# Taking the recurrent gates of two channel chunks together at every second step

## The chip, the cores and the metric

The kernel runs on one core of a Trainium2 chip. The metric is the device time of one execution in microseconds (us). TensorE does the matrix multiplications, VectorE and ScalarE the element-wise work and the evacuation of PSUM, GpSimd a few products, and SyncE's queue issues the loads of the weights. In the rows PE is TensorE, PEld its weight loads, DVE VectorE, ACT ScalarE, POOL GpSimd and SP SyncE.

## What is computed

One decoder layer on 512 tokens of width 1024, in float32. The part that matters here is the recurrent branch:

```python
xc = _causal_conv(x_rnn, conv_w, conv_b)                    # four taps over time
r = sigmoid(einsum('bshi,hij->bshj', xb, w_rg) + b_rg)      # 16 blocks of 64 channels
i = sigmoid(einsum('bshi,hij->bshj', xb, w_ig) + b_ig)
log_a = -8 * r * softplus(-lam)
a = exp(log_a); mult = sqrt(-expm1(2 * log_a))
h = associative_scan(a, mult * (i * xc))
y_a = (h * gelu(g_rnn)) @ w_rnn_proj
```

Beside it there are an attention branch (y_b, whose output projection is done during the recurrent branch), two gates that weigh the branches, an output projection, an MLP with a hidden width of 4096 and a gated embedding at the end.

## The kernel before

Activations lie transposed, 128 channels on the partitions and 512 tokens along the free axis, so 1024 channels are eight chunks of 128. Every weight comes as a unit of 128 x 1024 numbers, enough for one output chunk: `wload` (L123) has three units prepared ahead, and for each new unit SyncE's queue issues a load into `wr`, ScalarE copies it to a rounded `wh` (L118) and VectorE takes the remainder `wl` (L119). One output chunk is 24 matmuls in `proj` (L149): eight inner chunks times three products (wh with the high and the low part of the activation, L145 and L146, and wl with the high part, L147). So the third matmul of a unit is the first that needs its `wl`.

The order of TensorE, ScalarE, SyncE and GpSimd is the order of the program text (`manual_schedule`, L80). VectorE's order is laid out by the framework's scheduler, at build time, from what it expects to be ready. ScalarE has no spare order: an instruction that waits holds everything that the text puts behind it.

The stage that changes is the loop at L692, ten steps m = 0 to 9, with these parts:

- a projection `px{m}` of the recurrent input for m < 8, on TensorE;
- `x_scale` (L621): VectorE takes px out of PSUM into `xb`, ScalarE makes the first tap of the convolution, `xc` (L625);
- from m = 2 on, `gate_unit(m - 2)` (L639): six matmuls of 64 x 128 weights into two PSUM banks of the pair `tr` (two halves of the contraction, 64 rows each, L648), and four sigmoids of 64 x 512 on ScalarE (L654, L655);
- `x_conv` (L628): three taps on VectorE (L632), then the split of xc into a high part (ScalarE, L131) and a low part (VectorE, L132);
- one sigmoid of a gate of the attention branch, or four in steps 8 and 9 (L719);
- from m = 2 on, `wload` and `proj` of `pyb{m-2}`, the attention branch's projection, with `gate_post` (L658: a product on GpSimd, a Tanh on ScalarE) between them.

After every second chunk the pair's Exp stands on ScalarE (`decay_exp`, L665), in the next step its VectorE operations and Sqrt (`decay`, L669), and a step later its scans (L678). Exp, Sqrt and the sigmoids each need another function table on ScalarE (ACT_TABLE_LOAD). The last chunk's gates are taken in step 9 after `pyb7`, right before the loop over the eight projections `pgl{m}` (L737), whose results are multiplied with the scans' outputs.

PSUM has eight banks: four for projections (`mm`), two `tr`, and two in one tile `S` for the attention scores, whose last use is before this loop.

Of the kernel before, what the change touches and what calls it, by code (L numbers as in the profile page):

```python
# [9 lines left out]
F32 = mybir.dt.float32  # L10
F32R = mybir.dt.float32r
AF = mybir.ActivationFunctionType
# [4 lines left out]
P = 128  # L17
S = 512
D = 1024
KC = D // P  # L20
# [21 lines left out]
V_GMIX, V_GMLP, V_GPLE, V_CB, V_BRG, V_BIG, V_LAM, V_CW = 0, 8, 16, 24, 32, 40, 48, 56  # L42
# [8 lines left out]
LAG = 2  # L51
# [19 lines left out]
def layer_kernel(ctx, tc, w_all, x_t, p_t, vecs, row, ctab, out_t):  # L71
    nc = tc.nc
# [19 lines left out]
    def ftile(name):  # L92
        return act.tile([P, S], F32, tag="f", name=name, bufs=F_BUFS)

    def mm_ps(name):
        return ps.tile([P, S], F32, tag="mm", name=name, bufs=4)

    def tr_ps(name):
        return ps.tile([P, S], F32, tag="tr", name=name, bufs=2)
# [9 lines left out]
    def wsplit(u, pool, bufs, parts=1):  # L109
        raw = wp.tile([P, 1024], F32, tag="wr", name=f"wr{u}", bufs=2)  # L110
        wh = pool.tile([P, 1024], F32R, tag="wh", name=f"wh{u}", bufs=bufs)
        wl = pool.tile([P, 1024], F32R, tag="wl", name=f"wl{u}", bufs=bufs)
        n = 1024 // parts
        cuts = [slice(i * n, (i + 1) * n) for i in range(parts)]
        for c in cuts:
            nc.sync.dma_start(raw[:, c], w_all[u][:, c])
        for c in cuts:
            nc.scalar.activation(wh[:, c], raw[:, c], AF.Copy)  # L118
            nc.vector.tensor_tensor(out=wl[:, c], in0=raw[:, c], in1=wh[:, c].bitcast(F32),  # L119
                                    op=ALU.subtract)  # L120
        return wh, wl

    def wload(u):  # L123

        while u not in ready or (order and len(ready) <= AHEAD):
            wissue()
        return ready.pop(u)
# [21 lines left out]
    def proj(out, w, acts, ks=range(KC), kcs=KC, w0=0, t=slice(0, S)):  # L149

        wh, wl = w
        for k in ks:
            c = slice(w0 + k * P, w0 + (k + 1) * P)
            a = chunk(acts, k)
            mm3(out, wh[:, c], wl[:, c], a[:, 0, t], a[:, 1, t], k == 0, k == kcs - 1)
# [19 lines left out]
    def col(v, m):  # L175
        return vec[:, v + m : v + m + 1]
# [53 lines left out]
    def s_ps(name):  # L230
        return ps.tile([P, 4, 256], F32, tag="S", name=name, bufs=1)
# [240 lines left out]
    def p_transpose(u, g):  # L472
        sm, _ = probs[u, g]
        pt = tr_ps(f"ppt{u}{g}")
        for i in range(4):
            nc.tensor.transpose(pt[:, i * P : (i + 1) * P], sm[:, i, :], ident)
        p_t_[u, g] = pt

    def p_evac(u, g):
        pt = p_t_.pop((u, g))  # L480
        n = window(u)[1]
        for kb in range(n):
            prt = ftile(f"pt{u}{g}{kb}")
            if n == 1:
                nc.scalar.activation(prt, pt, AF.Copy)
            else:
                nc.vector.tensor_tensor(out=prt.rearrange("p (i t) -> p i t", t=P),
                                        in0=pt.rearrange("p (i t) -> p i t", t=P),
                                        in1=heads4(keep[kb]), op=ALU.mult)
            p_t_[u, g, kb] = prt  # L490

    def pv(u):
        po = mm_ps(f"po{u}")
        b0, nb = window(u)
        for kb in range(nb):
            for g in range(2):
                kv = 2 * (u // NB) + g
                nc.tensor.matmul(po[g * HD : (g + 1) * HD, :],
                                 vt[:, b0 + kb, kv * HD : (kv + 1) * HD],
                                 p_t_.pop((u, g, kb)), start=kb == 0, stop=kb == nb - 1)  # L500
        return po.rearrange("p (i t) -> p i t", t=P)

    def o_split(u, po):
        t = slice(u % NB * P, (u % NB + 1) * P)
        oj = o[u // NB]
        nc.scalar.activation(oj[:, :, 0, t], po, AF.Copy)
        nc.vector.tensor_tensor(out=oj[:, :, 1, t], in0=po, in1=oj[:, :, 0, t].bitcast(F32),
                                op=ALU.subtract)
# [108 lines left out]
    rnn = None  # L617
    hr = [None] * KC
    conv, gw, batch = {}, [], []

    def x_scale(m, px):  # L621
        xb = ftile(f"xb{m}")
        nc.vector.tensor_tensor(out=xb, in0=px, in1=rb, op=ALU.mult)
        xc = rnn.tile([P, S], F32, tag="h", name=f"xc{m}", bufs=KC)
        nc.scalar.activation(xc, xb, AF.Identity, bias=col(V_CB, m), scale=col(V_CW + 24, m))  # L625
        conv[m] = xb, xc

    def x_conv(m):  # L628
        xb, xc = conv[m]
        for j in range(3):  # L630
            sft = 3 - j
            nc.vector.scalar_tensor_tensor(  # L632
                out=xc[:, sft:], in0=xb[:, : S - sft], scalar=col(V_CW + 8 * j, m),
                in1=xc[:, sft:], op0=ALU.mult, op1=ALU.add)
        xr = rnn.tile([P, 2, S], F32R, tag="xr", name=f"xr{m}", bufs=3)
        split(xc, xr)
        conv[m] = xc, xr

    def gate_unit(m):  # L639


        xc, xr = conv.pop(m)
        halves = [slice(0, HD), slice(HD, P)]
        pgs = [tr_ps(f"pg{m}_{j}") for j in range(2)]
        c = slice(m * P, (m + 1) * P)
        for i, (w, part) in enumerate(((0, 0), (0, 1), (1, 0))):
            for pg, rows in zip(pgs, halves):
                nc.tensor.matmul(pg, gw[w][rows, c], xr[rows, part, :],  # L648
                                 start=i == 0, stop=i == 2)
        r = ftile(f"r{m}")  # L650
        ig = rnn.tile([P, S], F32, tag="ig", name=f"ig{m}", bufs=4)
        for j, pg in enumerate(pgs):
            own, other = halves[j], halves[1 - j]
            nc.scalar.activation(r[own], pg[own], AF.Sigmoid, bias=col(V_BRG, m)[own])  # L654
            nc.scalar.activation(ig[own], pg[other], AF.Sigmoid, bias=col(V_BIG, m)[other])  # L655
        return m, xc, (r, ig)

    def gate_post(m, xc, both):  # L658
        r, ig = both
        nc.gpsimd.tensor_tensor(out=ig, in0=ig, in1=xc, op=ALU.mult)  # L660

        nc.scalar.activation(xc, r, AF.Tanh, scale=cs[:, 0, m : m + 1])
        batch.append((m, r, ig, xc))
# [24 lines left out]
    def att_evac(m, py):  # L688
        nc.vector.tensor_tensor(out=gb[m], in0=py, in1=gb[m], op=ALU.mult)

    py_last = None
    for m in range(KC + LAG):  # L692
        if m < KC:
            w = wload(U_X + m)
            px = mm_ps(f"px{m}")
            proj(px, w, xg, range(0, 4))
            if m == 0:
                p_transpose(7, 1)
                p_evac(7, 1)
            proj(px, w, xg, range(4, 8))  # L700
            if m == 0:
                po = pv(7)
                o_split(7, po)
                att_scope.close()
                rnn = rnn_scope.enter_context(tc.tile_pool(name="rnn", bufs=1))
                gw += wsplit(U_GATE, rnn, 1)
        if py_last:
            att_evac(*py_last)
        for f in later.pop(0):
            f()  # L710
        later.append([])
        if m < KC:
            x_scale(m, px)
        if LAG <= m < KC + LAG - 1:
            g = gate_unit(m - LAG)
        if m < KC:
            x_conv(m)
        for gt in gb[m : m + 1] or ga[4 * (m - KC) : 4 * (m - KC) + 4]:
            nc.scalar.activation(gt, gt, AF.Sigmoid)  # L719
        if m >= LAG:  # L720
            w = wload(U_ATT + m - LAG)
            py_last = m - LAG, mm_ps(f"pyb{m - LAG}")
            if m < KC + LAG - 1:
                gate_post(*g)
            proj(py_last[1], w, o)
            if m == KC + LAG - 1:
                gate_post(*gate_unit(m - LAG))
        if len(batch) == 2:
            pair = list(batch)
            batch.clear()  # L730
            decay_exp(pair)
            later[0].append(partial(decay, pair))
            later[1] += [partial(scan, *p) for p in pair]
# [3 lines left out]
    for m in range(KC):  # L737
        w = wload(U_G + m)
        pg = mm_ps(f"pgl{m}")
# [15 lines left out]
    for m in range(KC):  # L755
        w, py = first[m] if m < 2 else (wload(U_RNN + m), mm_ps(f"pya{m}"))
# [13 lines left out]
    for m in range(KC):  # L770
        w = wload(U_OUT + m)
# [16 lines left out]
    for grp in range(4):  # L788
        us = rtiles(f"u{grp}_")
        for m in range(KC):  # L790
            w = wload(U_MLP + 16 * grp + m)
# [11 lines left out]
        for m in range(KC):  # L803
            w = wload(U_MLP + 16 * grp + 8 + m)
# [9 lines left out]
    for m in range(KC):  # L814
        if m % 4 == 0:
            w = wload(U_PLE + m // 4)
# [11 lines left out]
    for m in range(KC):  # L828
        w = wload(U_PG + m)
        parts = 2 if m == KC - 1 else 1  # L830
        for i in range(parts):
            pg = mm_ps(f"ppg{m}_{i}")
# [87 lines left out]
```

## Time and profile before

| | us |
|---|---|
| median of 3 runs | 849.38 (849.28 to 849.86) |
| the profiled execution, its own time | 850.14 |
| its span, first to last instruction | 847.7 |
| granted TensorE clock, mean | 0.999 |
| TensorE busy | 835.4 |
| VectorE busy | 524.5 |
| ScalarE busy | 363.9 |

The page gives the share of busy time of each engine over the whole span. A timeline gives for each instruction its start and duration in us from the start of the span, and in brackets how long its engine had idled before it and which instruction ended that. The ends of matmuls are modelled, so their starts are what is read.

### The profile page before, as it was taken

How to read it: one execution, taken by the hardware profiler on the slowest of the kernel's cores; microseconds unless marked ns; L12 is line 12 of the kernel's file. 1: busy time of each engine (PE TensorE's matmuls, PEld its weight loads, DVE VectorE, ACT ScalarE, POOL GpSimd, SP SyncE). 2: the span in 40 equal slices, each digit the busy share in tenths (PEclk: the TensorE clock that was granted, in tenths of full speed). 3: DMA queues.
4: the chain of work that ended last, by engine and by line, in shares of the span. 5: the costliest groups of instructions: out<-in, count | busy, mean ns of one | idle time of the engine just before them, and what ended most of it. 6: DMA issues, size and time to landing. Idle time of an engine off the chain costs nothing.

```text
span 847.7 us, 9949 instructions
## 1 busy us (share of the span) xinstructions
PE 835.4 (99%) x3798; PEld 679.7 (80%) x3798; DVE 524.5 (62%) x763; ACT 363.9 (43%) x583; POOL 103.0 (12%) x127
## 2 busy tenths in 40 slices
PE   9999999999999999999999999999999999999997
PEld 7878777777778788888888888888888888888886
DVE  5677787787678858675557633564355435555374
ACT  7334665555488896433343222222222222233431
POOL 2811422232011110000120000000000000002100
PEclk9999999999999999999999999999999999999999
DMA  7334212112233222334433232223322322332231
GB/s 248 124 98 152 70 55 75 50 63 66 71 102 96 77 75 80 118 124 149 140 109 101 98 113 92 95 99 100 100 86 92 121 95 80 99 100 100 75 124 51
DMA packets 25743, 83.99 MB, mean 99 GB/s; under 512 B 3040, under 2 KB 3424, under 8 KB 25696
## 3 DMA queue, kind: packets, MB, share of 16 engines
q1 hardware_dynamic: 25552, 83.32, 29.5%
q8 instruction: 30, 0.49, 0.3%
q14 instruction: 17, 0.14, 0.1%
q10 hardware_dynamic: 144, 0.05, 0.0%
HBM read 80.20 MB, written 2.10 MB: 97 GB/s over the span
## 4 chain that ended last, share of the span: by engine, by line
PE 92%; DVE 3%; DMA 2%; ACT 1%; POOL 1%; issue 1%; SPq 0%; ACTq 0%; POOLq 0%
PE pu L145 7%; PE pd L145 7%; PE pu L146 7%; PE pd L147 7%; PE pd L146 7%; PE pu L147 7%; PE pgate L145 4%; PE pgate L147 3%; PE pgate L146 3%; PE pq L246 2%; DMA wr<-in_w_all 2%; PE pyb L145 2%; PE S L424 2%; PE pgl L145 2%; PE ppg L145 2%; PE ppg L146 2%
## 5 line engine op out<-in xcount | busy, mean ns | idle before, releaser
L119 DVE TENSOR_TENSOR wl<-wr,wh 128x1024 fp32r<-128x1024 f32 (+1 forms) x144 | 180.6, 1256 | 58.3 <-ACT wh L118 58.1
L118 ACT ACTIVATE wh<-wr 128x1024 fp32r<-128x1024 f32 (+1 forms) x144 | 150.2, 1045 | 126.3 <-PE pd L146 98.4
L145 PE MATMUL pu<-x1g,wh 128*128 128x512 f32 x256 | 100.0, 391 | 0.0
L146 PE MATMUL pu<-x1g,wh 128*128 128x512 f32 x256 | 99.6, 389 | 0.0
L147 PE MATMUL pu<-x1g,wl 128*128 128x512 f32 x256 | 99.6, 389 | 0.0
L145 PE MATMUL pd<-u,wh 128*128 128x512 f32 x256 | 99.6, 389 | 0.0
L146 PE MATMUL pd<-u,wh 128*128 128x512 f32 x256 | 99.6, 389 | 0.0
L147 PE MATMUL pd<-u,wl 128*128 128x512 f32 x256 | 99.6, 389 | 0.0
L131 ACT ACTIVATE u<-up 128x512 fp32r<-128x512 f32 x32 | 20.2, 632 | 126.5 <-DVE up L798 126.5
L206 POOL TENSOR_TENSOR sq<-sq,sq_x 128x512 f32<-128x512 f32 x14 | 18.2, 1299 | 455.9 <-ACT sq_x L204 455.9
L807 DVE TENSOR_TENSOR xr<-pd,xr 128x512 f32<-128x512 f32 x32 | 22.1, 691 | 81.4 <-PE pd L147 81.4
L145 PEld LDWEIGHTS pu<-x1g,wh 128*128 128x128 f32 x256 | 48.0, 188 | 10.2 <-issue 0.2
L146 PEld LDWEIGHTS pu<-x1g,wh 128*128 128x128 f32 x256 | 48.1, 188 | 10.1 <-issue 0.2
L147 PEld LDWEIGHTS pd<-u,wl 128*128 128x128 f32 x256 | 48.0, 188 | 10.1
L147 PEld LDWEIGHTS pu<-x1g,wl 128*128 128x128 f32 x256 | 48.0, 188 | 10.1
L145 PEld LDWEIGHTS pd<-u,wh 128*128 128x128 f32 x256 | 48.0, 188 | 9.9
L146 PEld LDWEIGHTS pd<-u,wh 128*128 128x128 f32 x256 | 48.0, 188 | 9.9
L145 PE MATMUL pgate<-xg,wh 128*128 128x512 f32 x128 | 51.4, 402 | 0.0
L147 PE MATMUL pgate<-xg,wl 128*128 128x512 f32 x128 | 50.2, 392 | 0.0
L146 PE MATMUL pgate<-xg,wh 128*128 128x512 f32 x128 | 50.0, 391 | 0.0
L797 DVE TENSOR_TENSOR up<-pu,rb_x 128x512 f32<-128x512 f32 x32 | 22.1, 691 | 40.0 <-PE pu L147 40.0
L468 POOL TENSOR_SCALAR sm<-sm,st 128x128 f32<-128x128 f32 x64 | 30.1, 488 | 100.7 <-DVE st L466 45.6
(217 smaller groups left out, 1634.6 us busy)
## 6 DMA issues: line engine op xcount, KB each, us to landing
wr<-in_w_all SPq DMA_DIRECT2D x142, 512.0 KB, 3.3
x<-in_x_t SPq DMA_DIRECT2D x8, 256.0 KB, 5.1
xr<-in_x_t SPq DMA_DIRECT2D x8, 256.0 KB, 3.6
out<-pgt SPq DMA_DIRECT2D x7, 256.0 KB, 2.0
kt<-kt SPq DMA_DIRECT2D x8, 128.0 KB, 2.3
wr<-in_w_all SPq DMA_DIRECT2D x2, 256.0 KB, 3.3
pk<-in_p_t SPq DMA_DIRECT2D x2, 256.0 KB, 3.7
tab<-in_ctab SPq DMA_DIRECT2D x1, 384.0 KB, 6.6
```

The lines of the kernel that those rows point to most:

```text
L118: nc.scalar.activation(wh[:, c], raw[:, c], AF.Copy)
L119: nc.vector.tensor_tensor(out=wl[:, c], in0=raw[:, c], in1=wh[:, c].bitcast(F32), op=ALU.subtract)
L131: nc.scalar.activation(r[:, 0, :], src, AF.Copy)
L145: nc.tensor.matmul(out, ah, bh, start=start, stop=False)
L146: nc.tensor.matmul(out, ah, bl, start=False, stop=False)
L147: nc.tensor.matmul(out, al, bh, start=False, stop=stop)
L206: nc.gpsimd.tensor_tensor(out=acc, in0=acc, in1=t, op=ALU.add)
L246: nc.tensor.matmul(banks[n], a[:, part, n * P : (n + 1) * P], w[:, c], start=k == 0 and i == 0, stop=k == KC - 1 and i == 2)
L424: nc.tensor.matmul(pss[:, i, :], q_t[u][:, i % 2, 2 * g + i // 2, :], kt[part][:, kv, b0 * P : b0 * P + 256], start=part == 0, stop=part == 1)
L468: nc.gpsimd.tensor_scalar(out=sm[:, i, :], in0=sm[:, i, :], scalar1=den[:, i : i + 1], scalar2=1.0, op0=ALU.mult, op1=ALU.mult)
L797: nc.vector.tensor_tensor(out=y, in0=pu, in1=r1, op=ALU.mult)
L807: nc.vector.tensor_tensor(out=x1[m], in0=pd, in1=x1[m], op=ALU.add)
```

## The change

Where the loop took the gates of chunk m - 2 in each step from 2 to 9, it takes those of chunks m - 3 and m - 2 in the steps 3, 5, 7 and 9. All twelve matmuls stand together, then all eight sigmoids. The first chunk of a pair keeps the two `tr` banks, the second has the two banks of the score tile. The two calls of `gate_post` follow where the one stood. In step 9 the gates stand ahead of `pyb7`, where the last chunk's stood behind it.

```diff
-    def gate_unit(m):
+    def gate_units(ms):
-        xc, xr = conv.pop(m)
         halves = [slice(0, HD), slice(HD, P)]
-        pgs = [tr_ps(f"pg{m}_{j}") for j in range(2)]
-        c = slice(m * P, (m + 1) * P)
-        for i, (w, part) in enumerate(((0, 0), (0, 1), (1, 0))):
-            for pg, rows in zip(pgs, halves):
-                nc.tensor.matmul(pg, gw[w][rows, c], xr[rows, part, :],
-                                 start=i == 0, stop=i == 2)
-        r = ftile(f"r{m}")
-        ig = rnn.tile([P, S], F32, tag="ig", name=f"ig{m}", bufs=4)
-        for j, pg in enumerate(pgs):
...
-        return m, xc, (r, ig)
+        wide = s_ps(f"pg{ms[1]}").rearrange("p a b -> p (a b)")
+        banks = [[tr_ps(f"pg{ms[0]}_{j}") for j in range(2)], [wide[:, 0:S], wide[:, S : 2 * S]]]
+        units = []
+        for m, pgs in zip(ms, banks):
+            xc, xr = conv.pop(m)
+            c = slice(m * P, (m + 1) * P)
+            for i, (w, part) in enumerate(((0, 0), (0, 1), (1, 0))):
+                for pg, rows in zip(pgs, halves):
+                    nc.tensor.matmul(pg, gw[w][rows, c], xr[rows, part, :],
+                                     start=i == 0, stop=i == 2)
+            units.append((m, xc, pgs))
+        done = []
+        for m, xc, pgs in units:
+            r = ftile(f"r{m}")
+            ig = rnn.tile([P, S], F32, tag="ig", name=f"ig{m}", bufs=4)
+            for j, pg in enumerate(pgs):
+                own, other = halves[j], halves[1 - j]
+                nc.scalar.activation(r[own], pg[own], AF.Sigmoid, bias=col(V_BRG, m)[own])
+                nc.scalar.activation(ig[own], pg[other], AF.Sigmoid, bias=col(V_BIG, m)[other])
+            done.append((m, xc, (r, ig)))
+        return done
...
-        if LAG <= m < KC + LAG - 1:
-            g = gate_unit(m - LAG)
+        units = gate_units((m - 3, m - 2)) if m > LAG and m % 2 else []
...
-            if m < KC + LAG - 1:
+            for g in units:
                 gate_post(*g)
             proj(py_last[1], w, o)
-            if m == KC + LAG - 1:
-                gate_post(*gate_unit(m - LAG))
```

## Rows read from the trace of the kernel before

**Rows 1.** The page, busy time of each engine over the span.

```profile
PE 835.4 (99%) x3798; PEld 679.7 (80%) x3798; DVE 524.5 (62%) x763; ACT 363.9 (43%) x583; POOL 103.0 (12%) x127
```

**Rows 2.** Windows, two stretches: length, then busy us (count) of PE, PEld, DVE, ACT, POOL.

```profile
270.40:294.40 24.00, 24.00 (x109) 18.61 (x107) 20.65 (x26) 20.50 (x28) 3.10 (x3) 1.00 0.27 88
294.40:307.40 13.00, 13.00 (x62) 9.97 (x61) 10.38 (x14) 12.84 (x19) 2.33 (x2) 1.00 0.13 40
```

**Rows 3.** TensorE's timeline at chunk 0's gates, and the first matmul of pyb2.

```profile
227.58 0.39 PE L147 MATMUL px<-xg,wl 128*128 128x512 f32 x1
227.90 0.50 PE L648 MATMUL pg<-xr,wh 64*128 64x512 f32 x2
228.24 0.40 PE L648 MATMUL pg<-xr,wh 64*128 64x512 f32 x2
228.47 0.40 PE L648 MATMUL pg<-xr,wl 64*128 64x512 f32 x2
228.80 0.50 PE L145 MATMUL pyb<-o,wh 128*128 128x512 f32 x1
229.14 0.40 PE L146 MATMUL pyb<-o,wh 128*128 128x512 f32 x1
...
252.79 0.50 PE L145 MATMUL pyb<-o,wh 128*128 128x512 f32 x1
```

**Rows 4.** TensorE's timeline: start of pyb7, third matmuls of pgl1 and of pgl4.

```profile
300.91 0.39 PE L145 MATMUL pyb<-o,wh 128*128 128x512 f32 x1
...
313.36 0.39 PE L147 MATMUL pgl<-xg,wl 128*128 128x512 f32 x1
...
329.68 0.41 PE L147 MATMUL pgl<-xg,wl 128*128 128x512 f32 x1
```

**Rows 5.** VectorE's timeline there: wl of pgl1, evacuation of pyb6, wl of pgl4.

```profile
308.95 1.22 DVE L119 TENSOR_TENSOR wl<-wr,wh 128x1024 fp32r<-128x1024 f32 x1 [2.46 <-ACT wh L118]
310.10 0.68 DVE L689 TENSOR_TENSOR gate<-pyb,gate 128x512 f32<-128x512 f32 x1
...
328.32 1.21 DVE L119 TENSOR_TENSOR wl<-wr,wh 128x1024 fp32r<-128x1024 f32 x1
```

**Rows 6.** ScalarE's timeline at the end of the loop: chunk 7's Tanh, pgl4's wh.

```profile
316.62 0.72 ACT L662 ACTIVATE xc<-r,cs 128x512 f32<-128x512 f32 x1 [1.40 <-POOL ig L660]
...
326.66 1.04 ACT L118 ACTIVATE wh<-wr 128x1024 fp32r<-128x1024 f32 x1
```

**Rows 7.** ScalarE's timeline: wh of pyb2, L625 of the chunks 3, 4, 5 and 7.

```profile
238.77 1.06 ACT L118 ACTIVATE wh<-wr 128x1024 fp32r<-128x1024 f32 x1 [0.47 <-DMA wr<-in_w_all]
241.72 0.82 ACT L625 ACTIVATE xc<-xb,vec 128x512 f32<-128x512 f32 x1 [1.89 <-DVE xb L623]
...
254.87 0.81 ACT L625 ACTIVATE xc<-xb,vec 128x512 f32<-128x512 f32 x1 [0.84 <-DVE xb L623]
...
256.99 0.69 ACT L654 ACTIVATE r<-pg,vec 64x512 f32<-64x512 f32 x1
...
259.82 0.63 ACT L131 ACTIVATE xr<-xc 128x512 fp32r<-128x512 f32 x1
...
266.02 0.82 ACT L625 ACTIVATE xc<-xb,vec 128x512 f32<-128x512 f32 x1 [2.35 <-DVE xb L623]
...
290.30 0.81 ACT L625 ACTIVATE xc<-xb,vec 128x512 f32<-128x512 f32 x1 [2.35 <-DVE xb L623]
```

**Rows 8.** VectorE's timeline: wl of pyb2, xb of chunk 3, taps of chunks 4 and 5.

```profile
239.86 1.23 DVE L119 TENSOR_TENSOR wl<-wr,wh 128x1024 fp32r<-128x1024 f32 x1 [0.92 <-ACT wh L118]
241.01 0.68 DVE L623 TENSOR_TENSOR xb<-px,rb_x 128x512 f32<-128x512 f32 x1
...
258.99 0.74 DVE L632 SCALAR_TENSOR_TENSOR xc<-xb,vec,xc 128x511 f32<-128x511 f32 x1
...
263.03 2.35 DVE L119 TENSOR_TENSOR wl<-wr,wh 128x1024 fp32r<-128x1024 f32 x2
...
266.87 2.32 DVE L632 SCALAR_TENSOR_TENSOR xc<-xb,vec,xc 128x509 f32<-128x509 f32 x3 [0.89 <-ACT xc L625]
```

More of the change, by code (lines that the diff above doesn't have):

```diff
@@ L637, in x_conv @@
         conv[m] = xc, xr
-    def gate_unit(m):
-        xc, xr = conv.pop(m)
+    def gate_units(ms):
         halves = [slice(0, HD), slice(HD, P)]
-        pgs = [tr_ps(f"pg{m}_{j}") for j in range(2)]
-        c = slice(m * P, (m + 1) * P)
-        for i, (w, part) in enumerate(((0, 0), (0, 1), (1, 0))):
-            for pg, rows in zip(pgs, halves):
-                nc.tensor.matmul(pg, gw[w][rows, c], xr[rows, part, :],
-                                 start=i == 0, stop=i == 2)
-        r = ftile(f"r{m}")
-        ig = rnn.tile([P, S], F32, tag="ig", name=f"ig{m}", bufs=4)
-        for j, pg in enumerate(pgs):
-            own, other = halves[j], halves[1 - j]
-            nc.scalar.activation(r[own], pg[own], AF.Sigmoid, bias=col(V_BRG, m)[own])
-            nc.scalar.activation(ig[own], pg[other], AF.Sigmoid, bias=col(V_BIG, m)[other])
-        return m, xc, (r, ig)
+        wide = s_ps(f"pg{ms[1]}").rearrange("p a b -> p (a b)")
[19 more added lines that the diff above has]
+        return done
     def gate_post(m, xc, both):
```

## The prediction

> **What bounds the kernel now.** I read the page first: TensorE is busy for 835.4 of 847.7 us, so at first sight only its own work counts [rows 1]. Then the windows over the loop that is changed. TensorE is busy in all of it, at the full clock, but ScalarE is busy for 20.50 of 24.00 us in two steps of the loop, and for 12.84 of 13.00 at the loop's end [rows 2]. So there are two things to follow: what the change does for TensorE, and whether ScalarE, which prepares TensorE's weights, can still keep up.
>
> TensorE's timeline gives the first. Its plain step is the distance from the third matmul of pgl1 to that of pgl4, three units of 24 matmuls: (329.68 - 313.36)/72 = 0.2267 us [rows 4]. Around a gate unit, 1.56 us pass from the last matmul of px to the second of pyb (227.58 to 229.14) where two plain steps would take 0.45 [rows 3]. A gate unit so costs 1.11 us. Its six matmuls run as three pairs, which start 0.34 and 0.23 apart, so the work itself is 3 x 0.2267 = 0.68, and 0.43 go into the passage from 128-row to 64-row weights and back.
>
> The second comes from the timelines at the loop's end. The wl of pgl4 is finished by VectorE at 328.32 + 1.21 = 329.53 [rows 5], and the matmul that needs it starts at 329.68 [rows 4]: no slack at all. For pgl1 the slack is 313.36 - 310.17 = 3.2 us. In the middle of the loop there is plenty: the wl of pyb2 is ready at 241.09 [rows 8], and pyb2 starts at 252.79 [rows 3]. So whatever moves the wl of pgl4 later moves everything later, since TensorE has no idle time behind it in which to catch up; and TensorE can't keep a gain from the loop unless that wl comes earlier too.
>
> **The change part by part.**
>
> *TensorE.* Eight gate units with two passages each become four. With the second chunk's three pairs at 0.23 each, a double unit costs 1.11 + 0.68 = 1.79, and the saving is 4 x 0.43 = 1.7 us. If the passage from one chunk to the next cost as much as the first step after a passage (0.34 instead of 0.23 for each of three pairs [rows 3]), it would be 1.7 - 4 x 0.33 = 0.4. I take 1.7: the weights change between any two pairs as they do between the chunks. Two steps of the loop then take 4 x 24 x 0.2267 + 1.79 = 23.55 us instead of 23.98.
>
> *What costs nothing by itself.* The score tile's two banks have been free since the attention stage. No load is moved on SyncE's queue, and the matmuls wait for nothing new: chunk m - 3 is a step older than it was. The count of table loads stays at three in two steps, because the sigmoid of L719 stands in the even steps too. The GpSimd products come in pairs, but the Tanh that needs the second stands behind a gate sigmoid, a wh and the first Tanh. In step 9 this even removes a wait: chunk 7's Tanh waited 1.40 for its product [rows 6].
>
> *ScalarE.* Here is the price. From the L625 of chunk 3 to that of chunk 5, two steps, there are 266.02 - 241.72 = 24.30 us, with two waits of 0.84 and 2.35: 21.11 us of work, which the change only rearranges [rows 7]. What it rearranges are the covers. After L625, ScalarE must not do the split (L131) before VectorE has made three taps of the convolution. In an even step of before, the four sigmoids (256.99 to 259.82, 2.83 us) and their table load stand between the two and fill that time; the taps end at 258.99 + 0.74 = 259.73, and the split starts at 259.82 without a wait [rows 7, 8]. After the change nothing stands between them in even steps, so ScalarE waits for the taps, and behind the split are queued the gate sigmoid and the two wh of the next units. Call this wait W. Its lower bound is three taps alone, 2.32 and a hand-over, about 2.35 (as in step 5 [rows 8]); the upper one is the even step of before, where scans stand between the taps: 259.73 - 255.68 = 4.05 [rows 7, 8]. I take 4.05: the Sqrt of the pair still comes right before L625 in the even steps, so the scans become ready just then, as before.
>
> The odd steps have a wait X in front of L625, 2.35 before, because xb stood behind two wl on VectorE [rows 7, 8]. Afterwards px5 ends earlier and the two wh come later, so in order of readiness xb goes first and X is 0; if VectorE keeps its order, X stays at up to 2.35. I take 0. The start of the chain, A, is the L625 of chunk 3: 241.72 as before, if xb still stands behind the wl of pyb2 [rows 8], or 239.83, the end of that wh [rows 7]. I take 241.72, because that wl comes first in the program.
>
> *The sum.* L625 of chunk 7 then starts at B = A + 2 x (21.11 + W + X) = 241.72 + 2 x 25.16 = 292.04, instead of 290.30. From there to the end of the wl of pgl4 there were 329.53 - 290.30 = 39.23 us [rows 5, 7]. Four sigmoids and a Tanh of chunk 4, which stood ahead of B, now stand behind it (2.83 + 0.72), and the wait of 1.40 is gone [rows 6]: 41.38. The wl of pgl4 is ready at 292.04 + 41.38 = 333.42, 3.9 us later than before, and TensorE, which arrives 1.7 us earlier, stands still for some 5.6 us on the way, the first of it (about 1 us) at pgl1. TensorE's saving is then paid out in waiting. The profiled execution is at 850.14 (span 847.7 and 2.44 around it), 0.76 above the median; against the median the forecast is 849.38 + 3.9 = 853.3.
>
> The bounds by the same sum: B can't be before px7 is done. In before px7 ended at 287.87 (252.79 and 0.11, two units to the gates of chunk 3, and 23.98); five gate units of 1.11 ahead of it become two of 1.79, 1.97 less, and xb takes 0.68: 286.7. That gives 286.7 + 41.38 - 329.53 = -1.4. With A = 239.83 and the rest as taken it is +2.0; with X = 2.35 and A = 241.72, B = 296.74 and +8.6.
>
> **The rivals.**
>
> *The saving arrives.* If VectorE makes the taps without scans between them (W = 2.35) and takes xb at once, ScalarE needs 23.46 us for two steps, no more than TensorE's 23.55. From A = 239.83, B is then 286.75, and the time 848.0, at best 847.7 if TensorE keeps all of its 1.7. For it speaks that VectorE's order is laid out anew; against it that even steps of before have scans between the taps [rows 8]. It decides at B = 288.15, where the wl of pgl4 is as early as before. The Trainium skill, TensorEngine Tiling (Array Packing), section Tiling Modes, Key Properties, says that a change of the tiling mode drains TensorE: by that rule alone, half the changes give the whole 1.7 us. The trace agrees on the passages (0.43 each); what the page leaves out is who feeds TensorE afterwards.
>
> *VectorE keeps its order.* X stays at 2.35 and the time becomes 849.38 + 6.6 to 8.6 = 856.0 to 858.0. For it speaks that this order is not one of real readiness: at 308.95 VectorE had stood for 2.46 us before the wl of pgl1 [rows 5], while the evacuation of pyb6 stood behind it, whose matmuls were over when pyb7 began at 300.91 [rows 4]. The scheduler expects ScalarE earlier than it is. Against it: px5 is done 1.5 us earlier.
>
> *The passages don't get fewer in effect.* If TensorE saves only 0.4, the wl of pgl4 still sets the time: 853.3 again.
>
> **How the numbers follow.** The forecast, ScalarE late by 2 to 6 us (851.1 to 855.5): 0.50. VectorE's old order (855.5 to 858): 0.20. The saving arrives (847.5 to 849.4): 0.18. In between (849.4 to 851.1, from a shorter W or an early A): 0.12. About 0.2%, 1.7 us, is what a measurement here can tell from no change. TensorE's whole saving is just that, so of the 0.18 I put 0.07 below 847.7. Same holds the rest of it and the in-between, 0.23; slower 0.70. The range, 848.6 to 857.6, leaves out the best part of the saving and the latest case.
>
> **What would show it.** TensorE: four groups of twelve L648 matmuls, each about 1.8 us. ScalarE: the splits of chunks 4 and 6 wait about 4 us for L632, L625 comes 25 us apart, and that of chunk 7 lies near 292. TensorE's first matmuls with wl in pgl1 to pgl4 wait, 5 to 6 us together. Wrong would be: those splits wait 2.4 or less, or B is before 288.2, or VectorE takes scans ahead of xb.

## The result, and the profile after

The changed kernel takes 853.95 us (median of five runs, 852.83 to 854.23) against 849.38 (five runs, 849.09 to 849.86): a ratio of 1.0052, 95% interval 1.0041 to 1.0063. It is slower by 4.57 us where 3.9 were forecast. The profiled execution took 854.07 us with a span of 852.2.

The page of the kernel after, busy time of each engine and the chain that ended last:

```profile
PE 836.0 (98%) x3798; PEld 680.0 (80%) x3798; DVE 521.3 (61%) x763; ACT 364.1 (43%) x583; POOL 101.4 (12%) x127
...
PE 79%; ACT 8%; DVE 7%; DMA 3%; issue 2%; POOL 1%; SPq 0%; ACTq 0%; POOLq 0%
```

The first line hardly differs from [rows 1]: seen over the whole span, nothing happened. The second does. On the page of before this second line was:

```profile
PE 92%; DVE 3%; DMA 2%; ACT 1%; POOL 1%; issue 1%; SPq 0%; ACTq 0%; POOLq 0%
```

8% of the chain, some 68 us, now run over ScalarE, which is idle for 57% of the span; TensorE's share fell from 92 to 79%. So the loop is to be read by stretches.

Windows of the kernel after, with the columns of [rows 2] (behind POOL stand the granted clock, the DMA share and GB/s):

```profile
270.40:294.40 24.00, 24.00 (x111) 19.37 (x110) 18.48 (x25) 20.21 (x28) 2.59 (x2) 1.00 0.16 52
294.40:307.40 13.00, 12.39 (x59) 9.42 (x58) 8.26 (x13) 12.82 (x18) 2.96 (x2) 1.00 0.34 115
307.40:317.50 10.10, 10.10 (x45) 8.06 (x44) 6.19 (x8) 9.96 (x16) 1.88 (x2) 1.00 0.16 53
317.50:321.50 4.00, 1.39 (x6) 0.53 (x5) 1.23 (x1) 3.98 (x7) 0.70 (x1) 1.00 0.00 0
321.50:325.00 3.50, 3.50 (x9) 2.71 (x9) 1.71 (x4) 3.47 (x5) 0.00 (x0) 0.52 0.42 153
```

ScalarE (the fourth of the five) is full from 294.40 to 325.00: its gaps sum to 0.18 + 0.14 + 0.02 + 0.03 us. TensorE stands still for 0.61 in the second stretch and for 2.61 in the fourth, and in the fifth its granted clock is at 0.52.

TensorE's timeline after: one double gate unit, the double unit of step 9, and the places in pgl1, pgl2 and pgl4 where a matmul came late:

```profile
285.59 0.39 PE L147 MATMUL px<-xg,wl 128*128 128x512 f32 x1
285.91 0.73 PE L651 MATMUL pg<-xr,wh 64*128 64x512 f32 x4
286.48 0.40 PE L651 MATMUL pg<-xr,wl 64*128 64x512 f32 x2
286.71 0.62 PE L651 MATMUL pg<-xr,wh 64*128 64x512 f32 x4
287.18 0.40 PE L651 MATMUL pg<-xr,wl 64*128 64x512 f32 x2
287.50 0.50 PE L145 MATMUL pyb<-o,wh 128*128 128x512 f32 x1
287.84 0.40 PE L146 MATMUL pyb<-o,wh 128*128 128x512 f32 x1
...
300.41 0.50 PE L651 MATMUL pg<-xr,wh 64*128 64x512 f32 x2 [0.61 <-DVE xr L132]
...
312.67 0.50 PE L147 MATMUL pgl<-xg,wl 128*128 128x512 f32 x1
...
320.05 0.50 PE L145 MATMUL pgl<-xg,wh 128*128 128x512 f32 x1 [2.08 <-ACT wh L118]
320.39 0.39 PE L146 MATMUL pgl<-xg,wh 128*128 128x512 f32 x1
321.31 0.51 PE L147 MATMUL pgl<-xg,wl 128*128 128x512 f32 x1 [0.53 <-DVE wl L119]
321.64 0.60 PE L145 MATMUL pgl<-xg,wh 128*128 128x512 f32 x1
322.04 0.63 PE L146 MATMUL pgl<-xg,wh 128*128 128x512 f32 x1
322.47 0.63 PE L147 MATMUL pgl<-xg,wl 128*128 128x512 f32 x1
...
334.03 0.50 PE L147 MATMUL pgl<-xg,wl 128*128 128x512 f32 x1
```

TensorE's own part came true: from 285.59 to 287.84 pass 2.25 us, which is 1.80 more than two plain steps. Its losses come later. Counted from start to start, beyond a plain step for each matmul, they are 0.88 in step 9, 0.25 at pgl1, 3.15 at pgl2, 1.58 in eight matmuls that start some 0.42 apart instead of 0.23 (321.64 to 325.03), and 0.24 at pgl4: 6.10 in all. From the last px matmul of chunk 2 to the last matmul of the program it is 614.99 us in [rows 3]'s execution (227.58 to 842.57) and 619.43 here (227.57 to 847.00): 4.44 more, which is 6.10 less a saving of about 1.7.

ScalarE's timeline after, with the rows that answer to [rows 6] and [rows 7]:

```profile
231.89 0.80 ACT L625 ACTIVATE xc<-xb,vec 128x512 f32<-128x512 f32 x1
...
241.28 0.82 ACT L625 ACTIVATE xc<-xb,vec 128x512 f32<-128x512 f32 x1 [1.89 <-DVE xb L623]
...
261.17 0.63 ACT L131 ACTIVATE xr<-xc 128x512 fp32r<-128x512 f32 x1 [3.48 <-DVE xc L632]
...
267.73 0.82 ACT L625 ACTIVATE xc<-xb,vec 128x512 f32<-128x512 f32 x1 [2.08 <-DVE xb L623]
...
287.77 0.63 ACT L131 ACTIVATE xr<-xc 128x512 fp32r<-128x512 f32 x1 [3.57 <-DVE xc L632]
...
292.15 0.81 ACT L625 ACTIVATE xc<-xb,vec 128x512 f32<-128x512 f32 x1
...
318.95 1.04 ACT L118 ACTIVATE wh<-wr 128x1024 fp32r<-128x1024 f32 x1
```

The split of an even step, which did not wait in [rows 7], now waits 3.48 and 3.57 us for the taps. Chunk 7's L625 starts at 292.15 instead of 290.30, and at 318.95 comes the wh of pgl2 for which TensorE has been standing.

VectorE's timeline after (answering to [rows 5] and [rows 8]): xb in steps 5 and 7, and the wl of pgl2 and pgl4:

```profile
264.73 2.36 DVE L119 TENSOR_TENSOR wl<-wr,wh 128x1024 fp32r<-128x1024 f32 x2 [0.20 <-ACT wh L118]
267.01 0.68 DVE L623 TENSOR_TENSOR xb<-px,rb_x 128x512 f32<-128x512 f32 x1
...
291.05 0.67 DVE L623 TENSOR_TENSOR xb<-px,rb_x 128x512 f32<-128x512 f32 x1
291.63 2.35 DVE L119 TENSOR_TENSOR wl<-wr,wh 128x1024 fp32r<-128x1024 f32 x2
...
320.03 1.23 DVE L119 TENSOR_TENSOR wl<-wr,wh 128x1024 fp32r<-128x1024 f32 x1 [6.21 <-ACT wh L118]
...
332.76 1.22 DVE L119 TENSOR_TENSOR wl<-wr,wh 128x1024 fp32r<-128x1024 f32 x1
```

In step 5 xb still stands behind two wl, in step 7 ahead of them, but behind two scans (at 287.59 and 289.91), though px7's last matmul began at 285.59. The wl of pgl4 is ready at 333.98, 4.45 later than in [rows 5].

### The profile page after: what moved, and what is told of

Its sections match the earlier page's. It is cut to its first block, busy times and chain, and to the rows that moved or that the text cites. A ratio compares the mean times of both kernels' runs of the same rounds, so it can differ in the third digit from the quotient of the medians.

```text
span 852.2 us, 9944 instructions
## 1 busy us (share of the span) xinstructions
PE 836.0 (98%) x3798; PEld 680.0 (80%) x3798; DVE 521.3 (61%) x763; ACT 364.1 (43%) x583; POOL 101.4 (12%) x127
## 4 chain that ended last, share of the span: by engine, by line
PE 79%; ACT 8%; DVE 7%; DMA 3%; issue 2%; POOL 1%; SPq 0%; ACTq 0%; POOLq 0%
PE pu L147 7%; PE pd L147 7%; PE pu L145 7%; PE pd L146 7%; PE pd L145 7%; PE pu L146 7%; PE pgate L145 4%; PE pgate L147 3%; PE pgate L146 3%; PE pq L246 2%; DVE wl L119 2%; DMA wr<-in_w_all 2%; ACT wh L118 2%; PE S L424 2%; PE ppg L147 2%; PE ppg L145 2%
```

## The experiments

The theory, Q: TensorE gets its saving, but ScalarE's queue runs late, because the split waits for taps that nothing covers any more, and TensorE gives the saving back, and more, waiting for weights in pgl. The rivals: T, that TensorE itself loses by the double units; E, that only the new place of the last gates, at the loop's end, costs. Behind the change itself, the first four kernels ran on one chip, the next four on another, the last four on a third, each with its own runs of the kernel before. The last column is the account of TensorE as above, from the profiled executions: the distance from the last px matmul of chunk 2 to the program's last matmul, less the 614.99 of before.

| kernel | us | before, same chip | ratio, 95% | TensorE's distance |
|---|---|---|---|---|
| the change | 853.95 | 849.38 | 1.0052 (1.0041 to 1.0063) | +4.44 |
| cover | 854.89 | 849.46 | 1.0062 (1.0050 to 1.0075) | +5.91 |
| old_end | 855.18 | 849.46 | 1.0068 (1.0054 to 1.0082) | +5.96 |
| last_pair | 848.55 | 849.46 | 0.9992 (0.9983 to 1.0001) | -0.48 |
| order_only | 857.23 | 849.46 | 1.0091 (1.0077 to 1.0105) | +8.14 |
| mm_only | 851.55 | 849.70 | 1.0024 (1.0015 to 1.0034) | +2.22 |
| late_ga | 850.65 | 849.70 | 1.0018 (1.0009 to 1.0027) | +1.04 |
| cover_late_ga | 851.85 | 849.70 | 1.0027 (1.0016 to 1.0037) | +2.66 |
| before_late_ga | 849.18 | 849.70 | 0.9998 (0.9989 to 1.0007) | -0.06 |
| pinned | 849.91 | 849.35 | 1.0005 (0.9996 to 1.0014) | +0.46 |
| pinned_late_ga | 847.72 | 849.35 | 0.9978 (0.9969 to 0.9987) | -1.75 |
| mm_only_late_ga | 847.95 | 849.35 | 0.9981 (0.9972 to 0.9989) | -1.21 |
| before_plus | 851.04 | 849.35 | 1.0020 (1.0011 to 1.0029) | +2.22 |

**cover.** In even steps the convolution's taps and split move behind the weights' preparation, so that work stands on ScalarE between L625 and the split again.

```diff
-        if m < KC:
+        if m < KC and (m % 2 or m < LAG):
             x_conv(m)
...
             py_last = m - LAG, mm_ps(f"pyb{m - LAG}")
+            if m < KC and m % 2 == 0:
+                x_conv(m)
```

> The changed kernel, but in even steps the split of the convolution (and its three taps) stands behind the gate sigmoid and the wh of the next unit in program order; nothing else differs. Theory Q (ScalarE's queue is late because the taps are no longer covered in even steps, and the wl of pgl4 hands that on): ScalarE's waits for L632 in steps 4 and 6 fall from 3.5 us to under 1, L625 of chunk 7 starts at 286.8 to 288.5 instead of 292.15, and the time is 1.4 below to 0.5 above the kernel before (848.0 to 849.9). Rival T (TensorE itself loses: the double gate units in the score banks, its wait of 0.6 for the split of chunk 7, its clock at half speed): no change, 853.5 to 854.5. Rival E (the loss is made only at the loop's end, by the eight sigmoids ahead of the wh of pgl2): no change, about 854.

Q's number was missed, and by the number alone T and E, which expected about 854, come closer. The edit did half of what it was for, W fell to 1.11 in both even steps, but another wait took its place. ScalarE's timeline of this kernel in steps 4 and 5, and VectorE's ahead of xb:

```profile
260.81 0.64 ACT L131 ACTIVATE xr<-xc 128x512 fp32r<-128x512 f32 x1 [1.11 <-DVE xc L632]
266.73 0.82 ACT L625 ACTIVATE xc<-xb,vec 128x512 f32<-128x512 f32 x1 [4.34 <-DVE xb L623]
```

```profile
264.17 0.68 DVE L688 TENSOR_TENSOR ig<-xc,ig 128x512 f32<-128x512 f32 x1
264.89 1.23 DVE L689 TENSOR_TENSOR_SCAN xc<-r,ig 128x512 f32<-128x512 f32 x1
266.04 0.66 DVE L623 TENSOR_TENSOR xb<-px,rb_x 128x512 f32<-128x512 f32 x1
```

The scheduler put a scan and its product ahead of xb, in step 7 too (4.33). From chunk 2's L625 to chunk 7's pass 293.07 - 231.33 = 61.74 us, against 292.15 - 231.89 = 60.26 after the change and 58.40 before (290.30 - 231.90): the queue got later, and with it the kernel. The line of before that belongs to this, the L625 of chunk 2:

```profile
231.90 0.80 ACT L625 ACTIVATE xc<-xb,vec 128x512 f32<-128x512 f32 x1
```

**old_end.** Pairs in the steps 3, 5 and 7; chunk 6 alone in step 8, chunk 7 alone behind pyb7 as before. A single unit takes the two `tr` banks.

```diff
-        units = gate_units((m - 3, m - 2)) if m > LAG and m % 2 else []
+        units = []
+        if m in (3, 5, 7):
+            units = gate_units((m - 3, m - 2))
+        elif m == 8:
+            units = gate_units((6,))
...
             proj(py_last[1], w, o)
+            if m == KC + LAG - 1:
+                for g in gate_units((7,)):
+                    gate_post(*g)
```

> Chunks 0 to 5 in pairs as in the changed kernel, chunks 6 and 7 singly and where they stood before (step 8, and behind pyb7). Theory Q: the queue is as late as in the changed kernel when chunk 7's L625 comes (292.15); behind it come 39.23 us as before and chunk 4's sigmoids and Tanh (3.55): wl of pgl4 at 334.9, so 5 above the kernel before, 854 to 855.5. Rival E: the step-9 sigmoids are back behind the wh of pgl2, so the time is that of the kernel before less three saved passages, 848 to 849.4. Rival T: three quarters of the loss, about 852.8.

With the old end the kernel is still slow, and the number is Q's, but not in Q's way. The wl of pgl4 is about as late as Q had it (334.53), but no matmul waits for it: TensorE had lost its time earlier, in front of the single gate units, whose two PSUM banks ScalarE has not yet emptied (the view of waits from 222 to 335):

```profile
ACT xr L131 <- DVE xc L632: 16.9, 5, 3.6
...
PE pg L653 <- ACT ig L663: 4.6, 4, 1.9
```

The bank waits are of this edit's own making, so this run doesn't clear the new place of the last gates. The next one does.

**last_pair.** The opposite: single units in the steps 2 to 7, one pair in step 9.

```diff
-        units = gate_units((m - 3, m - 2)) if m > LAG and m % 2 else []
+        units = []
+        if LAG <= m < KC:
+            units = gate_units((m - 2,))
+        elif m == KC + LAG - 1:
+            units = gate_units((6, 7))
```

> Chunks 0 to 5 singly as in the kernel before, only chunks 6 and 7 as a pair in step 9. Theory Q: L625 of chunk 7 stays at 290.3, the wl of pgl4 is earlier by the product's wait of 1.4, and TensorE keeps one saved passage: 0.4 below the kernel before, 848.6 to 849.4. Rival E: all or most of the loss, 852 to 854. Rival T: a quarter of the loss, about 850.5.

Where the even steps keep their cover, a double unit and its banks cost nothing: TensorE does not wait in pgl, and its distance shortens by 0.48, one passage (0.43 by the prediction). Step 9 has the change's double unit and its eight sigmoids, so E, which put the loss there (852 to 854), falls. By the median the gain of 0.9 us can't be told from none.

**order_only and mm_only.** Two halves of the change. order_only has the six matmuls of one chunk in each step and the eight sigmoids of a pair in the odd steps; mm_only has the twelve matmuls in the odd steps and four sigmoids in each step, the second chunk's a step later. For both, `gate_units` is split into its matmuls (`gate_mm`, whose second argument picks the score banks) and its sigmoids (`gate_sig`); of each edit only the part in the loop is shown.

```diff
 # order_only
+        if LAG <= m < KC + LAG:
+            held.append(gate_mm(m - 2, m % 2 == 1))
+        if m % 2 and m > LAG:
+            units = [gate_sig(*g) for g in held]
+            held.clear()
 # mm_only
+        if m > LAG and m % 2:
+            held += [gate_mm(m - 3, False), gate_mm(m - 2, True)]
+        if m > LAG:
+            units = [gate_sig(*held.pop(0))]
+        if m == KC + LAG - 1:
+            units.append(gate_sig(*held.pop(0)))
```

> ScalarE's order as in the changed kernel (eight sigmoids in the steps 3, 5, 7, 9), but the matmuls of each chunk's gates in a step of their own as before (the odd-numbered chunks in the score banks), so that TensorE has eight passages again. Theory Q: as slow as the changed kernel, 853.3 to 855, since the saved passages were paid out in waiting. Rival T: like the kernel before, 849 to 850. Rival E: about 854.

> TensorE as in the changed kernel (twelve matmuls in the steps 3, 5, 7, 9), but four sigmoids in each step: the first chunk of a pair in the odd step, the second in the even step after it; chunks 6 and 7 both in step 9. Theory Q: the taps are covered again, L625 of chunk 7 comes at 289 to 291, and behind it stand chunk 4's sigmoids and Tanh (3.55 us) less the product's wait (1.4): 1 to 3 above the kernel before, 850.4 to 852.4. Rival T: as the changed kernel, 853.5 to 854.5. Rival E: as the changed kernel, since step 9 is the same.

order_only is the slowest of all, though it has single units like before: T, by which it should have been no slower than before, falls. But it is no clean half: VectorE took the two wl ahead of xb in both odd steps (X 2.08 twice), W was 4.00 and 3.92, and TensorE got a wait of its own for a bank:

```profile
296.17 0.79 PE L650 MATMUL pg<-xr,wh 64*128 64x512 f32 x1 [2.81 <-ACT ig L661]
```

So its 857.23, above Q's range, shows that the sigmoids' order with what it draws after it costs more than the whole loss, and not which share of the change's loss it is. In mm_only no split waits from chunk 3 on, and chunk 7's L625 comes 56.45 after chunk 2's (287.45 - 231.00), 288.34 on the scale of the change's trace and so a little earlier than Q's 289 to 291; the stall that is left is the wl of pgl4 (1.62) and the wh and wl of pgl2 (0.84 and 0.53). Its number is Q's. TensorE's double units and step 9 are the change's here, so T and E, by which it should have taken 853.5 or more, both miss.

**late_ga and its kin.** Four sigmoids in each of the steps 8 and 9, for the gates `ga` that are needed only in the later loop over pya, move there. late_ga does it to the change, cover_late_ga to cover, before_late_ga to before, mm_only_late_ga to mm_only.

```diff
-        for gt in gb[m : m + 1] or ga[4 * (m - KC) : 4 * (m - KC) + 4]:
+        for gt in gb[m : m + 1]:
             nc.scalar.activation(gt, gt, AF.Sigmoid)
...
     for m in range(KC):
+        nc.scalar.activation(ga[m], ga[m], AF.Sigmoid)
         w, py = first[m] if m < 2 else (wload(U_RNN + m), mm_ps(f"pya{m}"))
```

> The changed kernel with the eight gate sigmoids of the steps 8 and 9 (4.2 us on ScalarE) moved behind the pgl stage, to the eight pya units where their results are first used. Theory Q: the wl of pgl4 is ready 4.2 earlier, at 329.8: 0 to 0.6 above the kernel before, 849.4 to 850. Rival T: no change, 854. Rival E: as Q, 849.8.

> Both of these edits on the changed kernel: the split behind the gate sigmoid and wh in even steps, and the eight gate sigmoids in the pya units. Theory Q: the wl are all in time, TensorE keeps its four saved passages: 1.7 below the kernel before, 847.5 to 848.2. Rival T: 854. Rival E: 848 to 849.8.

> The kernel before with the eight gate sigmoids moved to the pya units, as a control. Theory Q: TensorE waits for nothing there, so no change, 849.2 to 849.6. Rivals: the same.

> 'mm_only' (double units on TensorE, four sigmoids in each step) with the eight gate sigmoids moved to the pya units. Theory Q: the wl of pgl4, 2.1 late in 'mm_only', comes 4.1 earlier and TensorE keeps its four saved passages: 1.2 to 1.8 below the kernel before (847.6 to 848.3). Rival T: no gain over 'mm_only', 851.5.

Twice four sigmoids of 2.19 us, 4.4 us less ahead of the weights, cut the change's loss from 4.57 to 0.95 us, and give before nothing: there was no wait to be ended. late_ga stayed a little above Q's 849.4 to 850. TensorE's timeline of late_ga tells why:

```profile
299.65 0.50 PE L651 MATMUL pg<-xr,wh 64*128 64x512 f32 x2 [0.50 <-DVE xr L132]
...
329.25 0.50 PE L147 MATMUL pgl<-xg,wl 128*128 128x512 f32 x1 [0.98 <-DVE wl L119]
...
355.57 0.50 PE L146 MATMUL pya<-y,wh 128*128 128x512 f32 x1 [0.22 <-DVE y L132]
```

Step 9 loses 0.77 from start to start, pgl4 1.25, pya 0.6: 2.6, less the 1.7 saved, makes 0.9, and 0.95 was measured. The third is new. The move alone doesn't make it: of the other kernels with this edit cover_late_ga has it, and before_late_ga, mm_only_late_ga and pinned_late_ga don't. cover_late_ga missed like cover (X 4.34 and 4.33 again). mm_only_late_ga, with a wait of only 0.24 left at pgl4, is faster than before.

**pinned and pinned_late_ga.** cover, with VectorE's order set by hand at the place that spoiled it: in steps 5 and 7 the scans come behind the last tap (`x_conv` is made to return it).

```diff
-        for f in later.pop(0):
-            f()
+        due = later.pop(0)
         later.append([])
+        if m not in (5, 7):
+            for f in due:
+                f()
...
+        if m in (5, 7):
+            with tc.issue_after(tap.ins):
+                for f in due:
+                    f()
```

> The run 'cover' with one thing more: the scans of chunks 0 to 3 are queued on VectorE behind the third tap of the odd step in which they fall (order of issue only), so that they stand neither between the taps nor ahead of xb. Theory Q: the waits of 4.3 us ahead of L625 in steps 5 and 7 fall to 2 or less and those for the taps in steps 4 and 6 to under 0.5, L625 of chunk 7 comes 3 to 5 us earlier than in 'cover', and the time is 0.8 below to 0.4 above the kernel before (848.7 to 849.9). Rival T (TensorE itself loses by the double units) and rival E (only the loop's end counts): as 'cover', about 854.5.

> 'pinned' with the eight gate sigmoids of the steps 8 and 9 moved to the pya units as well. Theory Q: no wl of the pgl stage is late, TensorE keeps its four saved passages: 1.2 to 1.8 below the kernel before (847.6 to 848.3). Rival T: 854. Rival E: 849.5 to 850.7, as 'late_ga'.

With the pin the splits of chunks 4 and 6 no longer wait at all, L625 of chunk 7 comes 56.24 after that of chunk 2 (288.28 - 232.04), and the time is again that of before (849.91, ratio 1.0005), at the upper end of what Q expected. T and E, which expected about 854.5, both fail: TensorE's double units and the loop's end are the change's. ScalarE's timeline of pinned, L625 of chunk 2, then split and L625 of the chunks 4 and 5, and 6 and 7:

```profile
232.04 0.80 ACT L625 ACTIVATE xc<-xb,vec 128x512 f32<-128x512 f32 x1
...
260.62 0.61 ACT L131 ACTIVATE xr<-xc 128x512 fp32r<-128x512 f32 x1
...
264.35 0.82 ACT L625 ACTIVATE xc<-xb,vec 128x512 f32<-128x512 f32 x1 [2.16 <-DVE xb L623]
...
283.95 0.62 ACT L131 ACTIVATE xr<-xc 128x512 fp32r<-128x512 f32 x1
...
288.28 0.81 ACT L625 ACTIVATE xc<-xb,vec 128x512 f32<-128x512 f32 x1 [2.76 <-DVE xb L623]
```

X did not fall to 2 or less as Q expected: it is 2.16 and 2.76, together 2.84 more than after the change. W is 7.05 less. With a wait of 0.29 in step 6 that makes 3.92, nearly all of the 4.02 by which the stretch from chunk 2 to chunk 7 is shorter (60.26 - 56.24). So W's end is what brings the time back, against a longer X.

B is also the point from which the prediction's first rival was to be decided: it put B at 288.15, and here it is at 231.89 + 56.24 = 288.13 on the scale of the change's trace. From there to the wl of pgl4 it is 41.83 (328.89 + 1.22 - 288.28), as after the change. The pin was not put on the kernel before; before_late_ga, though, shows that ScalarE running 4.4 us earlier gives that kernel nothing. One wait is left, which late_ga's edit ends. TensorE's timeline of pinned:

```profile
330.17 0.50 PE L147 MATMUL pgl<-xg,wl 128*128 128x512 f32 x1 [1.51 <-DVE wl L119]
```

and the window over the whole end of pinned_late_ga:

```profile
270.00:345.00 75.00, 75.00 (x341) 61.04 (x340) 62.18 (x79) 58.26 (x76) 7.57 (x5) 1.00 0.27 85
```

TensorE never waits there, and its distance is shorter by 1.75 us, as the four passages of 0.43 promised. The kernel is faster than the change and than before, by 1.63 us against before.

**before_plus.** The kernel before, with three useless copies of 128x512 on ScalarE in step 9, ahead of the weights' preparation; nothing that is used changes.

```diff
+        if m == KC + 1:
+            for _ in range(3):
+                nc.scalar.activation(gb[0], gb[0], AF.Copy)
```

> The kernel before with three Copy activations of 128 x 512 in place on ScalarE in step 9, ahead of the wh of pgl2: 1.6 us of work that nothing needs. Theory Q (the wl of pgl4 has no slack, TensorE catches up nowhere): 1.4 to 1.7 above the kernel before, 850.8 to 851.1. Rival (ScalarE is busy for 43% of the span, so such work hides): no change, 849.1 to 849.7.

The copies take 1.85 us of ScalarE's queue (311.17 to 313.02), and the kernel is 1.69 us longer by the median. TensorE's timeline shows a single wait, and it is at this matmul:

```profile
331.65 0.50 PE L147 MATMUL pgl<-xg,wl 128*128 128x512 f32 x1 [1.62 <-DVE wl L119]
```

So the wl of pgl4 had no slack before, as the prediction read from [rows 4, 5], and what was added to ScalarE's queue ahead of it came out nearly whole in the kernel's time.

## Why the prediction was right, and where it was not

**TensorE.** A double unit was to cost 1.79 and costs 1.80; the gain of 1.7 was to be there and to be paid out in waiting. pinned_late_ga shows it whole, 1.75, once ScalarE keeps up. The rival that the passages don't get fewer in effect (0.4) is refuted. The Trainium skill, TensorEngine Tiling (Array Packing), section Tiling Modes, Key Properties, says that a change of the tiling mode drains TensorE. The runs fit that in that each passage taken away gave back its 0.43; a drain itself is in no row.

**ScalarE's queue.** The mechanism was the predicted one, and B nearly exact, 292.15 for 292.04, but by terms that made up for one another. A was 0.44 earlier (241.28 for 241.72). W, taken at its upper bound of 4.05, was 3.48 and 3.57, together 1.05 less. The two steps' work was 20.89 (267.73 - 241.28 less the waits of 3.48 and 2.08) and 20.85 (292.15 - 267.73 less 3.57) instead of 21.11, 0.48 less. And X, taken as 0, was 2.08 in step 5 and 0 in step 7: 2.08 more. The sum of these is +0.11, so that B came out so close was luck. The rival "VectorE keeps its order" was half true; with X at 0 in both steps the same sum would have come 2.08 earlier. In order_only, X was 2.08 in both steps. One of the signs that the prediction named for being wrong did appear: VectorE took scans ahead of xb, in step 7 both (287.59 and 289.91). It cost nothing there, because ScalarE was still busy with two wh until L625 began at 292.15. What VectorE's scheduler will do was the least certain term in the working, and stayed so in the experiments: two kernels meant to cover W were spoiled by it, and one pinned place undid it.

**The path to pgl4.** From B to the end of its wl 41.38 were worked out and 41.83 passed; the wait of 1.40 for GpSimd went away as forecast. The 0.45 more and B's 0.11 are the 0.56 by which the wl came later than forecast (333.98 for 333.42). In the lower bound the terms given for px7's end add up to 287.76 and not to 287.87; that shifts the bound by 0.1 and touches no other sum.

**The stand-still.** 5.6 us were forecast, the first of it (about 1) at pgl1. Measured from start to start it is 6.10, but only 0.25 of that at pgl1 and 3.15 at pgl2, whose wh stands behind eight gate sigmoids and four of `ga` (from 311.27 to 318.95 on ScalarE); 0.88 in step 9, where the double unit waits for chunk 7's split, was not foreseen; and 1.58 is no wait but a lower clock. At pgl4 the matmul that needs the wl starts only 0.13 later than a plain step, so that the late pgl2 with its slow matmuls and the late wl of pgl4 end almost together. late_ga parts them: without the stall at pgl2 the wl of pgl4 still costs 1.25.

**What the page's first line does not tell.** TensorE is busy for 99% of the span, ScalarE for 43% [rows 1]. The Trainium skill, Perfetto Trace Analysis, section Identifying the Most-Contended Engine, says to find the engine with the highest occupancy and to optimise it first, and to judge TensorE's headroom by the share of its weight loads rather than of its matmuls. Over the whole span that is TensorE by either share (99% and 80%), and by that TensorE's 1.7 us were the thing to take; over the loop's end alone it is ScalarE, with 12.84 of 13.00 us against the weight loads' 9.97 [rows 2]. The 1.7 us were taken, and the kernel lost 4.57, because the engine that feeds TensorE has no slack in this one stage. Where both were done (pinned_late_ga, mm_only_late_ga), the gain arrived.

**Open.** Why VectorE's order comes out as it does in each kernel was seen only in its results; that the scheduler expects ScalarE earlier than it is remains an argument. No kernel changed W or X alone: pinned shows that W's end outweighs a longer X, and not how the change's loss divides between the two.

## What to carry to other kernels

Before instructions of an in-order engine are taken together, look at what each of them covers: here the moved sigmoids had filled the time in which ScalarE would otherwise wait for VectorE, and a wait of 3.5 us in every second step delayed all weights queued behind it. An engine's slack is to be read at the place where its product is consumed (end of the wl, start of the matmul), not from its busy share. And where another engine's order is laid out anew by a scheduler, look at that order first: a repair in the program text may come back as a new wait until that order is pinned.

## What was unexpected in the hardware

After TensorE had been busy for only 1.39 of 4.00 us at pgl2, its granted clock was 0.52 in the next 3.50 us, that is its lower level of 1.2 GHz, and 1.00 after that: the matmuls started some 0.42 apart instead of 0.23 (321.64 to 325.03), 1.58 us lost on top of the wait. Here it probably cost next to nothing, because the wl of pgl4, ready only at 333.98, would have held TensorE all the same. The same happened in cover, old_end and order_only. In order_only TensorE was busy for 1.15 of 4.00 us (from 293.00), and the granted clock was 0.51 from 298.00 to 303.00 and 1.00 after that. In cover and order_only TensorE waits for a wl later on (0.50 and 1.10), so that the loss is probably hidden there too; in old_end no wait follows. After the waits of 1.62 in mm_only and before_plus the matmuls went on 0.23 apart. The Trainium skill, TensorE: Matmul & The Clock Gate, Part 1, section "Wait — 56ns, not 53.3ns?", gives 426.7 ns from start to start at 512 columns for the cold array; the rows, 0.42 to 0.43, agree. So a stand-still can cost more than its length, and a forecast that lets TensorE wait has to leave room for it.
